# One flag of the tile scheduler: the same instructions, ordered by its timeline model instead of its core model

## The chip, the core and the metric

The kernel runs on one core of a Trainium2 chip. The time is that of one execution on the device, in microseconds (us). A NeuronCore has five engines with a queue each, taken in order: PE (TensorE, matmuls; PEld is its weight load), ACT (ScalarE), DVE (VectorE), POOL (GpSimd) and SP (SyncE, which here issues the DMAs).

## The reference

One inference step of one encoder layer, in float32, for 1024 tokens of a new prompt and 64 tokens of a stream that has 512 tokens in its caches:

```
h = x + 0.5 * rmsnorm(swiglu(rmsnorm(x, g_pre1), w_gate1, w_up1, w_down1), g_post1)
u = rmsnorm(h, g_premix) @ w_in      # split: c_q, c_kv, k_r | q_sb, k_sb, v_sb
o_mla = 8 heads of latent attention  # low-rank q and kv, rotary key, causal by chunks of 64
o_sb  = 8 heads of stick-breaking attention:
        z = q k * scale;  a = exp(log_sigmoid(z) + sum over later visible keys of log_sigmoid(-z))
h = h + rmsnorm(concat(headnorm(o_mla), headnorm(o_sb)) @ w_out, g_postmix)
h = h + 0.5 * rmsnorm(swiglu(rmsnorm(h, g_pre2), w_gate2, w_up2, w_down2), g_post2)
y = rmsnorm(h, g_final)              # and the new cache rows are returned
```

The width is 1024, the feed-forward width 2816.

## The kernel before

Features lie on the partitions, tokens on the moving axis. The tokens are two groups: group 1 holds 576 (the first half of the prompt and the sample, moved in chunks of 288), group 2 the other 512 (one chunk of 512). A float32 product is made of three matmuls of split operands (mm3, line 158: hi x hi, hi x lo, lo x hi), so each weight tile is loaded, split into wh and wl (lines 121 and 122) and used three times per chunk. Line 133 is the one line that issues every matmul, line 137 every transpose; so in the trace a matmul is told apart by its output tile.

The program writes two streams of work and weaves them. The mixing stream is, for one group, the end of the first feed-forward block (finish), the norm and input projections (premix, project), the attention (attend), and the output projection with its norm and residual (mix_out). Its PSUM tiles are called v, t and s, one buffer each (pool psa). The feed-forward stream computes the SwiGLU blocks (ffn, line 245); its PSUM tiles are called f, four buffers (pool psf). There are four feed-forward blocks in a row: the first of group 1, which runs alone (to about 430 us); block1, the first of group 2, woven with mix0, the mixing of group 1; block2, the second of group 1, woven with mix1, the mixing of group 2; block3, the second of group 2, at the end. Block2 needs the result of mix0 (prep2 scales it as its input), block3 that of mix1.

The weave (line 149) hands out the written order: after each step of the mixing stream it lets the feed-forward stream run until it has made SHARE times as much TensorE work:

```python
            while self.debt > 0 and next(second, None):
                self.debt -= self.work - mark
                mark = self.work
```

The written order is not yet the order on the engines. The tile context takes the whole program and schedules it: for each engine it takes, at each point of a modelled time, the instruction that is first in the written order among those whose operands and buffers are ready by the model. That fixes each engine's queue before the kernel runs; on the chip every engine takes its queue in order and waits where it must.

In the attention, a step computes the scores of 128 queries against n keys into the one tile s (scores, line 499), and then, for the stick-breaking heads (stick, line 510): a mask added on DVE (line 663), Abs, Exp and Ln on ACT (lines 517 to 519, of which 518 and 519 work on the copy a), a minimum with s on DVE (line 520), and one or two scans on DVE that read s again (lines 526 and 529). After the last reader of s the next scores may be written. The weights a are then turned by transposes into t, split (lines 563, 564) and multiplied with the values into v (weighted, line 545). The feed-forward stream's own VectorE work stands beside it: line 265 adds a down projection from f to y.

Of the kernel before, what the change touches and what calls it, by code (L numbers as in the profile page):

```python
# [15 lines left out]
P = 128  # L16
# [18 lines left out]
# token groups: (first token, tokens, chunk of the moving axis). The tokens lie as  # L35
# the first half of the prompt, the sample, the second half of the prompt.
# [4 lines left out]
# TensorE work of the feed-forward stream for one unit of the mixing stream's, part by part  # L41
# [8 lines left out]
class Layer:  # L50
    def __init__(self, tc, ctx, a):
        self.tc, self.nc, self.a = tc, tc.nc, a
        nc = self.nc
        self.const = ctx.enter_context(tc.tile_pool(name="const", bufs=1))
        nc.scalar.preload_act_table_set("natural_log_exp_and_others")
        self.turn = 0
        self.work = self.share = self.debt = 0.0
        self.pace = PACE
        self.mixed = False
        self.psf = ctx.enter_context(tc.tile_pool(name="psf", bufs=4, space=PSUM))  # L60
        self.psa = ctx.enter_context(tc.tile_pool(name="psa", bufs=1, space=PSUM))
        self.dram = ctx.enter_context(tc.tile_pool(name="dram", bufs=1, space=DRAM))
        c = self.const

        def load(name, shape, dt=F32):
            t = c.tile(list(shape), dt, name="c_" + name)
            nc.sync.dma_start(t, a[name])
            return t

        self.ones = c.tile([P, P], F32, name="ones")  # L70
        nc.vector.memset(self.ones, 1.0)
        self.eps = c.tile([P, 1], F32, name="eps")
        nc.vector.memset(self.eps, EPS)
        self.one = self.ones[:, 0:1]
        self.load = load

        def scratch(name, shape):
            return self.dram.tile(list(shape), F32, name=name)

        self.h1 = [scratch(f"h1_{g}", [P, KT, T]) for g, (_, T, _) in enumerate((G1, G2))]  # L80
        self.h2 = scratch("h2", [P, KT, G1[1]])
        self.o_s = [scratch(f"o_{g}", [D, T]) for g, (_, T, _) in enumerate((G1, G2))]
        self.qm = [scratch(f"qm_{g}", [HEADS, P, T]) for g, (_, T, _) in enumerate((G1, G2))]
        self.qs = [scratch(f"qs_{g}", [512, T]) for g, (_, T, _) in enumerate((G1, G2))]
        # keys and values: group 1 (prompt | new), group 2, cached
        self.kn = [scratch(f"kn_{g}", [512, T]) for g, T in enumerate((576, 512, 512))]
        self.kr = [scratch(f"kr_{g}", [32, T]) for g, T in enumerate((576, 512, 512))]
        self.ks = [scratch(f"ks_{g}", [512, T]) for g, T in enumerate((576, 512, 512))]
        self.vm = [scratch(f"vm_{g}", [T, 512]) for g, T in enumerate((576, 512, 512))]
        self.vs = [scratch(f"vs_{g}", [T, 512]) for g, T in enumerate((576, 512, 512))]  # L90
# [23 lines left out]
    # x = hi + lo exactly; without x, lo holds the value and is replaced in place  # L114
# [12 lines left out]
    # TensorE work is counted, for the interleaving of the two streams  # L127
# [15 lines left out]
    # a step without TensorE work in the first stream makes room for some of the second's  # L143
# [4 lines left out]
    # the steps of the first stream, with the second one's between them: self.share of its work each  # L148
# [15 lines left out]
    # a bank of the feed-forward stream  # L164
# [3 lines left out]
    # a bank of the mixing stream  # L168
# [10 lines left out]
    # sum of squares, tile by tile  # L179
# [9 lines left out]
    # 1 / sqrt(mean over all features + eps), on every partition, from the sums of squares  # L189
# [9 lines left out]
    # the same with the sums over the tiles left to TensorE (T at most 512)  # L199
# [10 lines left out]
    # tmp() gives [P, T] tiles  # L210
# [9 lines left out]
    # hi and lo of gain * src * r  # L220
# [7 lines left out]
    # y := res + gain * y * r, for one tile of features  # L228
# [76 lines left out]
    # projections of the mixing block for the tokens of one group  # L305
    def project(self, gi, g, hi, lo, pool, ev, tmp):
        nc, a = self.nc, self.a
# [13 lines left out]
        # query latent  # L321
# [13 lines left out]
        # rotary key: rows 64..95 the key, rows 96..127 its halves swapped  # L335
# [14 lines left out]
        # stick-breaking queries and keys, two heads per tile  # L350
# [16 lines left out]
        # latent attention: queries  # L367
        for m in range(2):
            # four heads: [query tile][head][128]
            wh, wl = self.weight(pool, a["wuq"][m])  # L370
            for h in range(4):
                e = tmp()
                for c0 in range(0, T, C):
                    cs = slice(c0, c0 + C)
                    ps = self.bank_m()
                    yield
                    for k in range(2):
                        ws = slice((k * 4 + h) * P, (k * 4 + h) * P + P)
                        self.mm3(ps[:, :C], wh[:, ws], wl[:, ws], cqh[:, k, cs], cql[:, k, cs], k == 0, k == 1)
                    nc.vector.tensor_tensor(e[:, cs], ps[:, :C], tab[:, cs], op=ALU.mult)  # L380
                nc.sync.dma_start(self.qm[gi][4 * m + h], e)
        # key/value latent
# [14 lines left out]
        # stick-breaking values, tokens on the partitions  # L397
# [17 lines left out]
        # latent attention: keys and values  # L415
# [3 lines left out]
    def cached(self, pool, ev, tmp):  # L419
        """keys and values of the cached latents"""  # L420
        nc, a = self.nc, self.a
        wh, wl = self.weight(pool, a["wukv"])
        cal = ev.tile([P, PAST], F32R, name="ll")
        cah = ev.tile([P, PAST], F32R, name="lh")
        ca = tmp()[:, :PAST]
        nc.sync.dma_start(ca, a["c_lat"])
        self.split(cah, cal, x=ca)
        yield from self.latent_kv(ev, tmp, wh, wl, cah, cal, PAST, PAST, 2)
# [25 lines left out]
    # ---- attention pieces  # L454
    def load_keys(self, pool, kind, h, parts):
        """hi and lo of the keys of one head on 128 rows."""
# [19 lines left out]
    def load_values(self, pool, pair, parts):  # L476
        """[128 keys, key tile, head, hi|lo, 64]"""
# [21 lines left out]
    def scores(self, ops, n):  # L499
        """ops: list of (lhsT, rhs tile); n keys in one or two equal halves."""  # L500
        nh = 1 if n <= 512 else 2
        w = max(n // nh, 256)
        ps = self.psa.tile([P, 2, 512], F32, name="s")
        for hf in range(nh):
            for i, (l, r) in enumerate(ops):
                self.mul(ps[:, hf, :w], lhsT=l, rhs=r[:, hf * w:hf * w + w],
                                      start=i == 0, stop=i == len(ops) - 1)
        return ps, nh, n // nh

    def stick(self, pool, ps, nh, w, n, mask):  # L510
        """weights of stick-breaking attention from the scores; the last key is never visible."""
# [9 lines left out]
        # minus the log weight: v[j] = (z[j+1] + v[j+1]) - log_beta[j]  # L521
# [23 lines left out]
    def weighted(self, pool, ab, v, h, tiles, o, par):  # L545
        """o[64*par .., 256] = sum over keys of value * weight, for two blocks of queries; the first block
        does not see the last tile of keys."""
# [40 lines left out]
    def headnorm(self, pool, o, n, row, gi, c0, sums=None, turned=None):  # L588
        """per-head RMSNorm of two heads on the partitions; sums or turned: eps * (softmax sum)^2 of each query."""
# [88 lines left out]
    def sum_rows(self, pool, total, nb):  # L678
        """eps * sum^2 of each query, repeated over the 64 rows of its head."""
# [9 lines left out]
    def sample_pair(self, pool, kind, pair):  # L689
# [9 lines left out]
        for par in range(2):  # L699
# [6 lines left out]
            # queries of this head in its own half of the columns, zeros in the other  # L706
# [54 lines left out]
        if mla:  # L761
            # row r of lhsT holds query r % 64 of head r // 64: only its own head's rows count
# [8 lines left out]
    # output projection, post norm, the residual (left in y), and the statistics of the next norm  # L771
# [30 lines left out]
def body(tc, a, ctx):  # L802
# [6 lines left out]
    # pool of the feed-forward stream  # L809
# [28 lines left out]
    def finish(gi, y, n, bank):  # L838
        """post norm and residual of a feed-forward block; after the second the final norm"""
# [18 lines left out]
    def last(gi, y, res, pool, step):  # L858
        """the same in steps of tokens, with the residual at hand"""
# [22 lines left out]
    def work(pool, T, n=4):  # L882
        """tiles for passing use, weights, and accumulators of the mixing stream"""
        class W:
            def tile(self, shape, dt, name):
                return pool.tile(shape, dt, name=name, bufs=2)
        return lambda: pool.tile([P, T], F32, name="e", bufs=n), W(), lambda: pool.tile([P, T], F32, name="acc")

    # first feed-forward block of group 1; the input norm of group 2 lies beside it
    T1, T2 = G1[1], G2[1]  # L890
    x1 = pair(fp, T2, "x")
    with tc.tile_pool(name="x0", bufs=1) as xp:
# [5 lines left out]
        for c0 in (0, half):  # L898
# [9 lines left out]
            # what the first half of the tokens suffices for  # L908
# [104 lines left out]
def layout(inp):  # L1013
    """The arrays of the launch: the inputs in the order the chip reads them, and constants of the shapes."""
# [14 lines left out]
    def tiles(w):  # [K, M] -> [M/128][128, K/128 * 128]  # L1029
# [22 lines left out]
    # constants  # L1052
# [15 lines left out]
def build(nc, arrays):  # L1068
# [5 lines left out]
    with tile.TileContext(nc) as tc:  # L1074
# [23 lines left out]
```

## Time and profile before

| | |
|---|---|
| median of 3 runs | 2368.2 us (2366.61 to 2371.72) |
| profiled execution, span from first to last instruction (no other time of it is given) | 2367.6 us |
| PE busy | 2283.5 us, 96% |
| DVE busy | 1539.0 us, 65% |
| ACT busy | 1244.7 us, 53% |
| POOL busy | 93.6 us, 4% |
| granted clock of TensorE, mean | 0.993 |

The profile is one execution. Busy time is that of an engine's instructions; a share of the span is a mean over stages. The granted clock is in parts of TensorE's full speed, 2.4 GHz; 0.50 is 1.2 GHz. In the views by windows each row is a stretch of the span.

### The profile page before, as it was taken

What the parts mean: (1) busy time and instruction counts of PE and PEld (TensorE: products, weight loads), DVE (VectorE), ACT (ScalarE), POOL (GpSimd) and SP (SyncE); (2) the same over time, 40 slices, a digit from 0 to 9 for tenths busy, and PEclk for the clock granted to TensorE, in tenths of its full rate; (3) what the DMA queues carried; (4) which work ended last, traced back from release to release, by engine and by line L of the source; (5) the groups of instructions that cost most, each with busy time, mean ns of one, the idle gap of its engine ahead of it and who ended that gap; (6) DMA issues with size and microseconds to landing.
All of it is one profiled execution on the core that took longest, in us unless ns stands there. A gap on an engine that the chain in (4) does not pass through costs nothing.

```text
span 2367.6 us, 37687 instructions
## 1 busy us (share of the span) xinstructions
PE 2283.5 (96%) x13869; PEld 2033.4 (86%) x13869; DVE 1539.0 (65%) x2743; ACT 1244.7 (53%) x2459; POOL 93.6 (4%) x270
## 2 busy tenths in 40 slices
PE   8999999989999999999999999999999999999997
PEld 7999999879987777788778999998888888888885
DVE  5555555764277878855873488888878588555555
ACT  6543333453367777754542477777776455433333
POOL 1000000010000000000110000000000010000001
PEclk9999999999999999999999999999999999999998
DMA  6322222445453343343444632323221424333321
GB/s 210 97 95 90 81 80 90 148 144 168 161 150 113 110 129 100 95 151 111 151 142 160 188 96 79 99 72 99 72 86 62 144 81 139 128 98 98 98 90 36
DMA packets 186615, 268.81 MB, mean 114 GB/s; under 512 B 59216, under 2 KB 68048, under 8 KB 186400
## 3 DMA queue, kind: packets, MB, share of 16 engines
q1 hardware_dynamic: 186432, 266.41, 35.8%
q8 instruction: 110, 1.80, 0.3%
q14 instruction: 73, 0.60, 0.1%
HBM read 227.61 MB, written 40.88 MB: 113 GB/s over the span
## 4 chain that ended last, share of the span: by engine, by line
PE 69%; DVE 12%; ACT 9%; DMA 4%; issue 4%; SPq 1%; POOL 1%; DVEq 0%; ACTq 0%; POOLq 0%
PE f L133 46%; PE s L133 11%; PE v L133 6%; PE t L133 3%; PE t L137 2%; DVE a L526 2%; DVE a L529 1%; ACT wh L121 1%; DVE a L520 1%; ACT a L517 1%; DVE wl L122 1%; ACT a L518 1%; ACT a L519 1%; DVE y L265 1%; DVE e L224 1%
## 5 line engine op out<-in xcount | busy, mean ns | idle before, releaser
L133 PE MATMUL f<-xh,wh 128*128 128x288 f32 (+1 forms) x2112 | 695.3, 329 | 4.4 <-ACT xh L121 2.8
L133 PE MATMUL f<-xl,wh 128*128 128x288 f32 (+1 forms) x2112 | 694.3, 329 | 2.9 <-POOL xl L122 1.8
L133 PE MATMUL f<-xh,wl 128*128 128x288 f32 (+1 forms) x2112 | 692.8, 328 | 0.0
L121 ACT CAST wh<-wr 128x512 fp32r<-128x512 f32 x638 | 374.2, 617 | 524.9 <-PE f L133 376.5
L122 DVE TENSOR_TENSOR wl<-wr,wh 128x512 fp32r<-128x512 f32 x638 | 431.2, 698 | 233.0 <-ACT wh L121 208.7
L133 PEld LDWEIGHTS f<-xl,wh 128*128 128x128 f32 x2112 | 397.7, 188 | 33.7 <-POOL xl L122 3.4
L133 PEld LDWEIGHTS f<-xh,wh 128*128 128x128 f32 x2112 | 397.6, 188 | 33.3 <-ACT xh L121 3.3
L133 PEld LDWEIGHTS f<-xh,wl 128*128 128x128 f32 x2112 | 397.5, 188 | 28.1 <-issue 0.8
L133 PE MATMUL f<-hh,wh 128*128 128x288 f32 (+2 forms) x1072 | 350.7, 328 | 6.6 <-ACT hh L121 3.2
L133 PE MATMUL f<-hl,wh 128*128 128x288 f32 (+2 forms) x1072 | 350.7, 327 | 0.0
L133 PE MATMUL f<-hh,wl 128*128 128x288 f32 (+2 forms) x1072 | 349.9, 327 | 0.2 <-DVE wl L122 0.2
L265 DVE TENSOR_TENSOR y<-f,y 128x288 f32<-128x288 f32 (+2 forms) x488 | 247.9, 523 | 85.4 <-PE f L133 83.8
L133 PEld LDWEIGHTS f<-hh,wh 128*128 128x128 f32 x1072 | 201.7, 189 | 23.4 <-ACT hh L121 4.0
L133 PEld LDWEIGHTS f<-hh,wl 128*128 128x128 f32 x1072 | 202.1, 189 | 14.3 <-issue 1.0
L133 PEld LDWEIGHTS f<-hl,wh 128*128 128x128 f32 x1072 | 202.1, 189 | 13.8 <-issue 0.8
L293 DVE TENSOR_TENSOR act<-f,act 128x288 f32<-128x288 f32 (+1 forms) x132 | 70.0, 531 | 92.6 <-PE f L133 91.8
L564 DVE TENSOR_TENSOR pl<-t,ph 128x384 fp32r<-128x384 f32 (+1 forms) x160 | 101.2, 633 | 35.6 <-ACT ph L563 31.2
L563 ACT CAST ph<-t 128x384 fp32r<-128x384 f32 (+1 forms) x160 | 86.7, 542 | 57.2 <-PE t L137 54.7
L292 DVE TENSOR_TENSOR act<-f,act 128x288 f32<-128x288 f32 (+1 forms) x132 | 69.8, 529 | 66.5 <-ACT act L291 66.4
L137 PE MATMUL t<-c_ident,a 128*128 128x128 f32 x616 | 106.0, 277 | 2.7 <-ACT a L531 0.9
L133 PE MATMUL s<-kh,qh 128*128 128x256 f32 (+3 forms) x224 | 84.4, 378 | 24.0 <-DVE a L529 16.1
L121 ACT CAST hh<-act 128x288 fp32r<-128x288 f32 (+1 forms) x132 | 64.8, 491 | 66.0 <-DVE act L293 65.9
(312 smaller groups left out, 3464.7 us busy)
## 6 DMA issues: line engine op xcount, KB each, us to landing
wr<-in_wg SPq DMA_DIRECT2D x176, 256.0 KB, 2.9
wr<-in_wu SPq DMA_DIRECT2D x176, 256.0 KB, 3.0
wr<-in_wd SPq DMA_DIRECT2D x176, 256.0 KB, 3.2
wr<-in_win SPq DMA_DIRECT2D x44, 256.0 KB, 3.3
kl<-ks SPq DMA_DIRECT2D x64, 128.0 KB, 2.8
wr<-in_wout SPq DMA_DIRECT2D x32, 256.0 KB, 2.8
h<-y SPq DMA_DIRECT2D x16, 288.0 KB, 2.3
p<-in_xT SPq DMA_DIRECT2D x16, 256.0 KB, 3.4
```

The lines of the kernel that those rows point to most:

```text
L121: nc.scalar.copy(hi, x)
L122: eng.tensor_tensor(lo, x, f(hi), op=ALU.subtract)
L133: self.nc.tensor.matmul(out, lhsT=lhsT, rhs=rhs, start=start, stop=stop)
L137: self.nc.tensor.transpose(out, x, ident)
L224: self.nc.vector.scalar_tensor_tensor(x, src(k), self.gain(name, k), r, op0=ALU.mult, op1=ALU.mult)
L265: nc.vector.tensor_tensor(yy, ps[:, :C], yy, op=ALU.add)
L292: nc.vector.tensor_tensor(s, pg[:, :C], s, op=ALU.mult)
L293: nc.vector.tensor_tensor(s, pu[:, :C], s, op=ALU.mult)
L517: nc.scalar.activation(av, z, AF.Abs)
L526: nc.vector.tensor_tensor_scan(a[:, j0:n - 1][:, ::-1], zz[:, ::-1], a[:, j0:n - 1][:, ::-1], BIG, op0=ALU.add, op1=ALU.subtract)
L563: nc.scalar.copy(ph[:, end:], tr[:, end:])
L564: nc.vector.tensor_tensor(pl[:, end:], tr[:, end:], f(ph[:, end:]), op=ALU.subtract)
```

## The change

The tile context is opened with a flag. Its scheduler then takes the time at which an instruction is ready from its timeline model, where it took it from its core model. The rest of the diff removes comments, without moving a line.

```diff
@@ -1071,7 +1071,7 @@
     for k, s in OUTS.items():
         a[k] = nc.dram_tensor("out_" + k, list(s), F32, kind="ExternalOutput").ap()
     a["xT"] = [a["xT0"], a["xT1"]]
-    with tile.TileContext(nc) as tc:
+    with tile.TileContext(nc, schedule_with_timeline_sim=True) as tc:
         with ExitStack() as ctx:
             body(tc, a, ctx)
```

The instructions are the same, 13688 on PE, 1247 on SP and 275 on POOL in both programs; 26 copies that may go to any engine move from DVE to ACT (2745 and 2393 before, 2719 and 2419 now). Their order differs on every engine. Numbers behind a tile's name count the tiles in the written order, the same in both programs.

First place: TensorE, in the attention of group 1, at the step v_8434 (the product of weights and values of one pair of heads). The tiles f_9278 and f_12538 belong to block1; f_12538 is its last one. In the order before:

```order
L133 MATMUL f_9278<-xl_99,wh_9257 128x512
L133 MATMUL f_9278<-xh_98,wl_9256 128x512
L133 MATMUL v_8434<-pl_8437,v_8382 128x256
L133 MATMUL v_8434<-ph_8436,v_8382 128x256
...
L133 MATMUL f_9278<-xh_98,wh_9257 128x512
```

And in the new order:

```order
L133 MATMUL f_12538<-hh_12372,wh_12443 128x512
L133 MATMUL f_12538<-hl_12373,wh_12443 128x512
L133 MATMUL f_12538<-hh_12372,wl_12442 128x512
L133 MATMUL v_8434<-pl_8437,v_8382 128x256
L133 MATMUL v_8434<-ph_8436,v_8382 128x256
...
L133 MATMUL s_8561<-kh_8550,qh_8556 128x256
L133 MATMUL s_8561<-kl_8549,qh_8556 128x256
L137 MATMUL t_8507<-c_ident_988,a_8497 128x128
```

Block1's matmuls from f_9278 to f_12538 stood behind v_8434 and now stand ahead of it; what follows v_8434 is scores and transposes of the attention.

Second place: TensorE, in the attention of group 2, at the transposes t_17196. The tiles f_18505 and f_21639 belong to block2; f_21639 is its last one. In the order before:

```order
L133 MATMUL f_18505<-xl_12460,wh_18427 128x288
L133 MATMUL f_18505<-xh_12459,wl_18426 128x288
L137 MATMUL t_17196<-c_ident_988,a_17156 128x128
L137 MATMUL t_17196<-c_ident_988,a_17108 128x128
...
L133 MATMUL v_17161<-pl_17176,v_16743 128x256
L133 MATMUL v_17161<-ph_17175,v_16743 128x256
...
L133 MATMUL s_17251<-kh_17079,qh_17089 128x512
```

And in the new order:

```order
L133 MATMUL f_21639<-hh_21381,wh_21510 128x288
L133 MATMUL f_21639<-hl_21382,wh_21510 128x288
L133 MATMUL f_21639<-hh_21381,wl_21509 128x288
L137 MATMUL t_17196<-c_ident_988,a_17156 128x128
L137 MATMUL t_17196<-c_ident_988,a_17108 128x128
...
L133 MATMUL v_17161<-pl_17176,v_16743 128x256
L133 MATMUL v_17161<-ph_17175,v_16743 128x256
...
L133 MATMUL s_17464<-kh_17451,qh_17459 128x320
L133 MATMUL s_17464<-kl_17450,qh_17459 128x320
```

Block2's matmuls from f_18505 to f_21639 now stand ahead of t_17196, and so does the score matmul s_17251, which followed it.

## Rows read from the trace of the kernel before

**Rows 1.** The page: span, and busy time, share of the span and instructions by engine.

```profile
span 2367.6 us, 37687 instructions
...
PE 2283.5 (96%) x13869; PEld 2033.4 (86%) x13869; DVE 1539.0 (65%) x2743; ACT 1244.7 (53%) x2459; POOL 93.6 (4%) x270
```

**Rows 2.** Windows, feed-forward alone: length, busy (count) by engine, clock, DMA share, GB/s.

```profile
core 0: us, PE busy (x) PEld busy (x) DVE busy (x) ACT busy (x) POOL busy (x), PEclk, DMA share, GB/s
118.40:177.60 59.20, 59.20 (x448) 59.20 (x448) 31.68 (x61) 24.19 (x52) 2.69 (x2) 1.00 0.30 95
2131.20:2190.40 59.20, 59.20 (x263) 48.99 (x262) 31.38 (x49) 20.25 (x37) 0.00 (x0) 1.00 0.31 98
```

**Rows 3.** Windows, only instructions on tile s: PE, PEld, DVE, ACT busy.

```profile
798.69:1026.75 228.06, 31.42 (x138) 20.62 (x138) 54.93 (x114) 22.82 (x60) 1.00 0.37 109
1622.59:1836.64 214.05, 30.59 (x118) 19.08 (x118) 64.76 (x82) 23.58 (x36) 1.00 0.24 75
```

**Rows 4.** Timeline of one turn of s: start, duration, engine, line, operation [wait].

```profile
893.87 0.47 PE L133 MATMUL s<-kh,qh 128*128 128x512 f32 x1 [0.25 <-DVE a L526]
...
898.16 0.69 DVE L265 TENSOR_TENSOR y<-f,y 128x512 f32<-128x512 f32 x1
...
900.13 0.35 PE L133 MATMUL s<-kh,qh 128*128 128x256 f32 x1 [0.42 <-DVE a L526]
```

**Rows 5.** Windows, only PE's instructions on tiles f.

```profile
798.69:1026.75 228.06, 159.62 (x619) 1.00 0.37 109
1026.75:1096.66 69.91, 17.32 (x75) 1.00 0.36 118
1096.66:1160.80 64.14, 59.22 (x252) 1.00 0.46 143
1622.59:1836.64 214.05, 138.19 (x951) 1.00 0.24 75
1836.64:1902.29 65.65, 19.86 (x142) 1.00 0.39 128
1902.29:1966.77 64.48, 57.97 (x409) 0.97 0.30 90
```

**Rows 6.** Windows, all instructions, columns as in rows 2.

```profile
430.00:798.69 368.69, 357.24 (x2097) 307.24 (x2095) 229.27 (x423) 198.49 (x425) 16.73 (x57) 1.00 0.47 148
798.69:1026.75 228.06, 221.44 (x1133) 173.94 (x1133) 180.03 (x360) 166.06 (x369) 10.73 (x73) 1.00 0.37 109
1026.75:1096.66 69.91, 69.74 (x465) 65.30 (x463) 32.00 (x51) 28.10 (x53) 0.00 (x0) 1.00 0.36 118
...
1160.80:1622.59 461.79, 446.54 (x2949) 409.35 (x2948) 331.44 (x571) 283.57 (x531) 18.53 (x62) 0.99 0.40 123
1622.59:1836.64 214.05, 203.11 (x1449) 189.77 (x1448) 172.04 (x303) 151.11 (x266) 6.13 (x42) 1.00 0.24 75
1836.64:1902.29 65.65, 63.80 (x337) 55.01 (x335) 32.81 (x57) 25.19 (x46) 0.00 (x0) 1.00 0.39 128
...
0.00:34.46 34.46, 25.68 (x103) 19.34 (x104) 20.11 (x38) 20.89 (x48) 8.18 (x12) 0.90 0.69 230
```

**Rows 7.** Timeline, PE: two score matmuls, and two sums of squares behind the residuals.

```profile
809.18 0.36 PE L133 MATMUL s<-kh,qh 128*128 128x256 f32 x1 [0.38 <-DVE a L526]
...
1136.17 0.75 PE L133 MATMUL s<-rx,ones 128*128 128x288 f32 x2 [2.21 <-DVE rx L187]
...
1628.94 0.39 PE L133 MATMUL s<-kh,qh 128*128 128x320 f32 x1
...
1931.88 0.65 PE L133 MATMUL t<-rx,ones 128*128 128x512 f32 x1
```

**Rows 8.** Groups on tile a from 798.69: count, then min/median/max ns.

```profile
L518 ACT ACTIVATE a<-a x25: 309/527/707, 798.3 to 1014.0; 128x384 f32<-128x384 f32 x6, 128x512 f32<-128x512 f32 x6, 128x128 f32<-128x128 f32 x5, 128x256 f32<-128x256 f32 x5
L519 ACT ACTIVATE a<-a,ones x25: 400/617/780, 798.9 to 1015.2; 128x384 f32<-128x384 f32 x6, 128x512 f32<-128x512 f32 x6, 128x128 f32<-128x128 f32 x5, 128x256 f32<-128x256 f32 x5
```

**Rows 9.** Windows around two drops of the granted clock, columns as in rows 2.

```profile
1192.00:1199.00 7.00, 2.50 (x18) 2.22 (x18) 7.00 (x12) 3.69 (x8) 1.44 (x1) 0.87 0.72 228
1199.00:1203.00 4.00, 4.00 (x12) 2.97 (x13) 2.97 (x7) 2.79 (x6) 0.00 (x0) 0.50 0.68 221
...
17.00:20.00 3.00, 2.97 (x9) 2.41 (x10) 3.00 (x7) 2.58 (x7) 1.45 (x2) 0.50 0.00 0
```

## The prediction

> **The bound.** I read the page first: TensorE is busy in 2283.5 us of a span of 2367.6 [rows 1]. That 96% would make any order of the same instructions worth nothing, and it is a mean over stages with different limits, so I went on to the windows. In two stretches that hold feed-forward work alone, TensorE is never idle and a matmul takes 59.20/448 = 0.132 us with 288 columns and 59.20/263 = 0.225 us with 512 [rows 2]. These are the prices of feed-forward work wherever it stands.
>
> Then I read the attention stretches by tile. The score tile s has one buffer, and it is handed from a score matmul to the mask, three ScalarE passes, a VectorE minimum and a scan, and only then to the next score matmul. Instructions on that tile alone take 31.42 us on TensorE, 54.93 on VectorE and 22.82 on ScalarE of the 228.06 us of group 1's last part of attention [rows 3]. One turn shows the pace: score matmul at 893.87, next at 900.13, started when the scan of line 526 ended, 6.26 us later, and in the turn stands one VectorE addition of the feed-forward stream, 0.69 us, between the steps of the chain [rows 4]. So attention advances at the pace of a chain in which TensorE has a small part, and TensorE reads as full only because feed-forward matmuls fill the rest of every turn. The reader should see two limits that lie on each other: TensorE's work and the score chain.
>
> **The change.** No instruction's work is added or removed; some 26 copies go from VectorE to ScalarE, which at about the 0.69 us of the addition in rows 4, on engines that other work keeps free for them, I cost at nothing (ends: 18 us either way, if all lay on one engine's path). What changes is the order. The two pieces of the order ahead show it: TensorE takes block1's feed-forward matmuls up to the last one (f_12538) before the attention step v_8434, and block2's up to the last one (f_21639) before t_17196. In the trace of before those steps start at 798.69 and 1622.59, and after them stand 619 + 75 + 252 = 946 feed-forward matmuls of block1 and 951 + 142 + 409 = 1502 of block2 [rows 5]. In the new order these lie ahead of that point, and behind it the attention goes on with nothing to fill its turns; the next block can't fill them, since block2 needs the result of mix0 and block3 that of mix1.
>
> *Work pulled ahead.* 946 x 0.2251 = 212.9 us, and 1502 x 0.1321 = 198.5 us. It is put into stretches where TensorE is already busy 357.24 of 368.69 us and 446.54 of 461.79 [rows 6], so there is room for 11.45 and 15.25 us at most. I take 8 and 10 as filled (ends: 0 and all of it). VectorE can follow: 229.27 us there, and 946/263 x 31.38 = 113 us more, in 574 us of time. The weights of the pulled matmuls are loaded ahead with them, on SP's queue; the DMA share is 0.31 in the dense stretch and 0.47 here, so neither is full.
>
> *What is left of the first stretch.* From 798.69 to 1160.80 were 362.1 us. In the new order they are replaced by four pieces in a row. The attention: the next score matmul in the new order is s_8561, which starts at 809.18 in the trace [rows 7], so 1026.75 - 809.18 = 217.6 us of attention remain. Without feed-forward work its turns get shorter. The one turn above gives (6.26 - 0.69)/6.26 = 0.89. The floor is the chain's own instructions with every hand-over at zero: 31.42 + 54.93 + 22.82 and the two passes of lines 518 and 519 that touch only its copy, 25 x (0.527 + 0.617) = 28.6 [rows 8], together 137.8 of 228.06, which is 0.60. The other end is 1.0. I take 0.85, near the turn, which has its hand-overs in it: 184.9 us. The output projection: 69.91 us [rows 6], with 17.32 us of feed-forward work in it [rows 5], of which I take off half (ends: none and all): 61.3. The statistics and the residual, one tile after another through a load, to the matmul at 1136.17: 40.3 [rows 7], TensorE hardly works there. The scaling of the next block's input, 8 tiles, each a multiplication and a split of about 0.7 us (the addition in rows 4 is the nearest): 10. Sum 296.5, so 65.6 us go. First stage: 212.9 - 8 - 65.6 = +139.3.
>
> *The second stretch* alike, from 1622.59 to 1966.77, 344.2 us: the attention from 1628.94 [rows 7] to 1836.64, 207.7 x 0.85 = 176.5; the projection 65.65 less half of 19.86, 55.7; the statistics to 1932.5, 30.2; the scaling 10. Sum 272.4, so 71.8 go. Second stage: 198.5 - 10 - 71.8 = +116.7.
>
> *The clock.* Around 1192 to 1199 TensorE is busy 2.50 us of 7.00, and in the next 4 us, busy throughout, its granted clock is 0.50, the level of 1.2 GHz; at the start of the kernel a like drop is seen [rows 9]. In the bare attention TensorE will be used as lightly: the matmuls that are not feed-forward take 221.44 - 159.62 = 61.8 us there, a third of 184.9. If all score matmuls of both stretches ran at half the clock, 31.42 + 30.59 = 62.0 us would be added; at full clock nothing. I take 10, since the matmuls there come every few us and the drops in the trace are short.
>
> The Trainium skill ("TensorE: Matmul & The Clock Gate", Part 1, on the gate) says that the throttled state is the default and that activity releases it. By the row alone the drop is an episode, and the sum stands; by the rule a lightly used engine stays throttled, and the sum would be 52 us higher. The trace bears the rule out in its direction: 0.50 behind a light stretch, 1.00 in every dense one. No row shows a long light stretch.
>
> *The start of the kernel.* The new order also exchanges weights and tokens of the first 35 us. TensorE is idle for 34.46 - 25.68 = 8.8 us there [rows 6]; ends: that much less, that much more; I take zero.
>
> *Sum:* 139.3 + 116.7 + 10 = +266.0 on the profiled span of 2367.6, which is 0.6 under the median of the runs: 2633.6, 2634 us. Nothing moves in the last block, which starts later by the whole sum.
>
> **Rivals.**
>
> *The clock stays low in both bare stretches.* The price is the 52 us not yet counted: 2686 us. For it: the rows at the low level, behind TensorE busy 36% [rows 9]. Against it: that light stretch itself was still granted 0.87 on average, and in the turns of the attention matmuls come a few us apart. Chance 0.13.
>
> *The bare chain is much faster,* because most of each turn is waiting behind feed-forward work on ScalarE and VectorE: a factor of 0.65 in place of 0.85, 0.20 x 425.3 = 85 us less, 2549. For it: the floor of 0.60. Against it: the turn of rows 4 holds one feed-forward operation between the chain's steps. Chance 0.07.
>
> *TensorE is the only bound, and the new order serves it better: faster.* The filled idle time, 11.45 + 15.25 = 26.7 us, would be won, and the attention behind would run at TensorE's own share, 61.8 and 203.11 - 138.19 = 64.9 us: 2341. It decides from where the bare attention takes no more than these 127 us of its 425, a factor of 0.30. Against it: half of the floor of the chain. Chance 0.03.
>
> *The order doesn't matter,* since the sum of TensorE's work is the same and the engines' queues even it out: 2368. TensorE takes its instructions in order, and the displaced ones depend on nothing that could slide back. Chance 0.02.
>
> **The numbers.** The forecast has 0.75. Its own range: factor 0.75 to 1.0 (-43 to +64), half of the projection's overlap (18.6 either way), recovered idle time (-9 to +18), the start (8.8 either way), the clock (-10 to +52). Not all fall on one side, so 2570 to 2725, which also holds the rival of the clock; outside lie the other three and a little of the upper end, some 0.17. A measurement of this kernel tells 0.2% (5 us) from no change. Faster by over that: 0.03, the third rival; within: 0.02; slower: 0.95.
>
> **Signs.** In the changed kernel's windows: a stretch of about 180 us in either attention without a single feed-forward matmul, TensorE busy about a third there; before it stretches at 97% and more that are 205 and 188 us longer; block2's first feed-forward matmul near 1300 (1160.80 now) and block3's near 2230 (1966.77 now). The granted clock in the bare stretches separates the first rival; the time of a turn, 5.3 us where it was 6.26, the second. The prediction is wrong if feed-forward matmuls run beside the attention to its end.

## The result, and the profile after

The changed kernel takes 2735.83 us (median of 4 runs, 2733.68 to 2737.0) where the kernel before takes 2368.24: a ratio of 1.1545, interval 1.1528 to 1.1561. The forecast was slower, 2634 us, with a range that ended at 2725; the loss is 367.6 us where 266 were forecast. Of the four runs of e8, below, one took 4615 us, and the time given for e8 is the median of the other three.

The page of the changed kernel, span and busy time as in [rows 1]:

```profile
span 2733.3 us, 37804 instructions
...
PE 2369.9 (87%) x13869; PEld 2129.1 (78%) x13869; DVE 1536.0 (56%) x2717; ACT 1272.0 (47%) x2485; POOL 102.3 (4%) x270
```

The other engines work as long as before. TensorE is busy 86 us longer at the same instructions, and idles 363 us where it idled 84. The windows of the changed kernel on tile f, as in [rows 5], show where:

```profile
430.00:1003.52 573.52, 400.37 (x1734) 0.99 0.42 132
1003.52:1339.48 335.96, 0.00 (x1) 0.63 0.22 66
1339.48:1993.23 653.75, 451.99 (x3168) 0.99 0.36 111
1993.23:2327.77 334.54, 0.00 (x0) 0.67 0.17 51
```

Two stretches of 336 and 335 us hold no feed-forward matmul. They begin with v_8434 (1003.52, was 798.69) and t_17196 (1993.23, was 1622.59) and end with the first matmul of block2 (1339.48, was 1160.80) and of block3 (2327.77, was 1966.77). The same stretches with all engines, as in [rows 6]; of each the attention, the projection, and the statistics with the scaling:

```profile
430.00:1003.52 573.52, 565.52 (x3069) 492.15 (x3068) 339.38 (x599) 281.34 (x571) 17.62 (x59) 0.99 0.42 132
...
1006.17:1224.77 218.60, 130.96 (x508) 101.01 (x508) 110.66 (x240) 113.98 (x270) 10.30 (x69) 0.58 0.18 48
1224.77:1294.83 70.06, 54.59 (x386) 53.94 (x387) 21.67 (x32) 25.98 (x50) 0.00 (x0) 0.86 0.32 103
1294.83:1339.48 44.65, 4.71 (x9) 1.98 (x9) 17.18 (x24) 9.87 (x17) 2.79 (x2) 0.50 0.29 93
1339.48:1993.23 653.75, 639.12 (x4450) 611.75 (x4450) 436.33 (x785) 360.95 (x691) 24.52 (x64) 0.99 0.36 111
1997.14:2214.10 216.96, 120.24 (x485) 98.29 (x486) 112.59 (x168) 108.77 (x168) 6.47 (x42) 0.64 0.09 26
2214.10:2282.62 68.52, 50.71 (x199) 38.90 (x200) 21.37 (x32) 25.84 (x44) 0.00 (x0) 0.83 0.33 104
2282.62:2327.77 45.15, 5.75 (x9) 1.72 (x8) 32.03 (x45) 15.39 (x27) 12.02 (x4) 0.56 0.23 74
2327.77:2733.30 405.53, 380.86 (x1696) 316.41 (x1696) 210.54 (x336) 146.16 (x268) 14.20 (x12) 0.97 0.27 89
```

The reader should see three things. Ahead of the bare stretches TensorE is full, at 98.6 and 97.8%. In the bare attentions VectorE is busy about half the time and ScalarE about half, and still they take 218.6 and 217.0 us, where the same steps with all the feed-forward work between them took 217.6 and 207.7 before. And the granted clock there is 0.58 and 0.64 in the mean, between the levels of 1.2 and 2.4 GHz; TensorE is busy 60 and 55% of the time, where the prediction's sign was a third.

On the score tile alone, the same steps before (809.18 to 1026.75 and 1628.94 to 1836.64) and in the changed kernel:

```profile
809.18:1026.75 217.57, 30.72 (x136) 20.29 (x136) 51.25 (x109) 22.24 (x59) 1.00 0.36 106
1628.94:1836.64 207.70, 28.88 (x112) 18.06 (x112) 63.43 (x80) 22.27 (x32) 1.00 0.24 74
```

```profile
1006.17:1224.77 218.60, 47.16 (x136) 32.17 (x136) 51.58 (x109) 22.18 (x59) 0.58 0.18 48
1997.14:2214.10 216.96, 42.82 (x112) 29.41 (x112) 63.81 (x80) 22.17 (x32) 0.64 0.09 26
```

VectorE and ScalarE spend the same time on it; TensorE spends 16.4 us more in the first attention and 13.9 in the second, at the lower clock. What is left between in the first, 217.57 - 104.21 = 113.4 us before, is 97.7 now: 15.7 us less. The two nearly cancel. Waits of TensorE in the first bare attention (waiter, what it waited for, us in total, times, longest):

```profile
PE s L133 <- DVE a L526: 39.9, 14, 5.7
PE t L137 <- DVE pl L564: 14.4, 8, 2.2
```

The score matmul waits for the scan, as it did before, but in the kernel before feed-forward matmuls filled these waits.

### The profile page after: what moved, and what is told of

It reads as the page before. It is cut to its first block, busy times and chain, and to the rows that moved or that the text cites. A ratio compares the mean times of both kernels' runs of the same rounds, so it can differ in the third digit from the quotient of the medians.

```text
span 2733.3 us, 37804 instructions
## 1 busy us (share of the span) xinstructions
PE 2369.9 (87%) x13869; PEld 2129.1 (78%) x13869; DVE 1536.0 (56%) x2717; ACT 1272.0 (47%) x2485; POOL 102.3 (4%) x270
## 5 line engine op out<-in xcount | busy, mean ns | idle before, releaser
L121 ACT CAST wh<-wr 128x512 fp32r<-128x512 f32 x638 | 362.5, 618 | 598.6 <-PE f L133 420.5
L122 DVE TENSOR_TENSOR wl<-wr,wh 128x512 fp32r<-128x512 f32 x638 | 417.4, 692 | 365.5 <-ACT wh L121 359.1
L137 PE MATMUL t<-c_ident,a 128*128 128x128 f32 x616 | 129.2, 329 | 71.9 <-DVE pl L564 51.8
L133 PE MATMUL s<-kh,qh 128*128 128x256 f32 (+3 forms) x224 | 100.3, 449 | 86.9 <-DVE a L529 40.5
L137 PEld LDWEIGHTS t<-c_ident,a 128*128 128x128 f32 x616 | 89.8, 167 | 100.4 <-DVE pl L564 32.7
L133 PE MATMUL v<-pl,v 128*128 128x256 f32 x320 | 113.2, 369 | 24.0 <-DVE pl L564 18.0
```

What stands on the lines that cost most here:

```text
L121: nc.scalar.copy(hi, x)
L122: eng.tensor_tensor(lo, x, f(hi), op=ALU.subtract)
L133: self.nc.tensor.matmul(out, lhsT=lhsT, rhs=rhs, start=start, stop=stop)
L137: self.nc.tensor.transpose(out, x, ident)
```

## Experiments

All were run beside the kernel before, whose median was 2366 to 2369 us each time; ratios are to it.

**e1: the work written ahead, core model.** The shares are changed, no flag.

```diff
-SHARE = (0.1, 1.5, 0.1, 0.1, 1.2, 0.1)
+SHARE = (0.35, 8.0, 0.1, 0.3, 4.0, 0.1)
```

> The core model orders the program, as in the kernel before; only the weave's shares are changed, so that the feed-forward stream is written as far ahead of the mixing stream as the new order has it (its matmuls of block1 and block2 end in the first and in the second attention at about the same step). Theory A (feed-forward work taken ahead leaves the rest of the attention bare, and that alone is the loss): 2700 to 2750 us, with two stretches of about 330 us without a feed-forward matmul. Theory C (the loss comes from something else in the new order: VectorE, ScalarE or the DMA queue): under 2450 us.

2763.8 us (1.168, 1.1663 to 1.1698). Its windows on tile f:

```profile
1009.60:1357.90 348.30, 0.00 (x0) 0.63 0.21 64
2012.60:2360.00 347.40, 0.00 (x0) 0.69 0.17 54
```

The time is 14 us over the range of theory A, and theory C is far off. The old scheduler model makes a loss of the same kind and a little more when the feed-forward stream is written as far ahead. Being far ahead is enough, without the flag.

**e2: the stream held back, with the flag.**

```diff
+        elif self.side == 2 and len(self.lead) > 0:
+            self.tc.add_manual_dep(ins.ins, self.lead[-1].name, mybir.DependencyInfo(
+                mybir.DependencyClass.NoSync, mybir.DependencyReason.DATA), reason="order")
-SHARE = (0.1, 1.5, 0.1, 0.1, 1.2, 0.1)
+SHARE = (0.1, 2.35, 0.1, 0.1, 1.75, 0.1)
```

> The flag stays on; each feed-forward matmul that is written between two steps of the mixing stream is queued behind the last mixing matmul written before it, and the shares of the two attentions are raised from 1.5 and 1.2 to 2.35 and 1.75, so that TensorE has the feed-forward work where the kernel before has it. All other engines keep the order that the timeline model gives. Theory A: 2350 to 2400 us. Theory C: over 2600 us.

2654.7 us (1.1216): theory A missed. The first attention took 467 us (711 to 1178) where it took 351 before (690 to 1041), with TensorE busy 381 and 343 of them. Either the ties leave TensorE's order worse than before, or the other engines' order costs; the run can't tell which, so the next pair ties the order exactly.

**e5, e6, e9 to e11: whole queues tied.** A table holds the order of an engine's instructions in one kernel; each is tied behind the one before it.

```diff
+    d = np.frombuffer(zlib.decompress(base64.b85decode(order)), np.int16).astype(int)
+    at = np.cumsum(d + 1) - 1
+    for p, q in zip(at, at[1:]):
+        tc.add_manual_dep(mine[q], mine[p].name, mybir.DependencyInfo(
+            mybir.DependencyClass.NoSync, mybir.DependencyReason.DATA), reason="order")
```

> The flag stays on, but TensorE's matmuls and transposes are tied, each behind the one before it, into exactly the order of the kernel before (a table of 13686 numbers); ScalarE, VectorE, GpSimd and the DMA queue are ordered by the timeline model around it. Theory A (TensorE's order alone makes the loss): 2360 to 2400 us. Theory C (the order that the timeline model gives the other engines makes the loss, as the 2655 us of the kernel with the stream held back would have it): 2600 to 2740 us. A number between them splits the loss.

> The reverse: the core model, with TensorE tied into exactly the order of the changed kernel. Theory A: 2700 to 2750 us. Theory C: under 2450 us.

> The flag with TensorE and ScalarE tied into the order of the kernel before; VectorE, GpSimd and the DMA queue are left to the timeline model. With TensorE alone tied it took 2551 us. Theory D1 (the 184 us left there come from ScalarE's queue: passes of the score chain behind work that isn't ready): under 2420 us. Theory D2 (they come from VectorE's queue): over 2500 us. Theory D3 (from the DMA queue, or both alike): between, or over 2500 in the next run too.

> The flag with TensorE and VectorE tied into the order of the kernel before; ScalarE, GpSimd and the DMA queue are left to the timeline model. D1: over 2500 us. D2: under 2420 us. D3: neither.

> The flag with TensorE, ScalarE and VectorE tied into the order of the kernel before; GpSimd, the DMA queue and the engine of 95 free copies are left to the timeline model. D1 and D2: 2360 to 2385 us. D3 with the DMA queue: over 2450 us.

| model | queues tied | us | ratio |
|---|---|---|---|
| flag | none (the changed kernel) | 2735.8 | 1.1545 |
| core (e6) | TensorE as in the changed kernel | 2730.9 | 1.1534, 1.1515 to 1.1554 |
| flag (e5) | TensorE as before | 2551.4 | 1.0779, 1.0758 to 1.0801 |
| flag (e9) | TensorE, ScalarE as before | 2476.9 | 1.0470, 1.0451 to 1.0488 |
| flag (e10) | TensorE, VectorE as before | 2481.5 | 1.0490, 1.0472 to 1.0507 |
| flag (e11) | all three as before | 2374.8 | 1.0037, 1.0023 to 1.0051 |

With TensorE's new order the time is within 5 us of the changed kernel's, whichever model orders the rest (e6, theory A): TensorE's order is enough to make the loss. The other engines were not held at their old order there; the core model laid theirs around TensorE's. Giving TensorE its old order back wins only half of the loss (e5, between the two theories): the order that the timeline model gives the other engines around it, which is not their order in the changed kernel either, costs 184 us. Some 70 to 75 of these go with ScalarE's old order alone or VectorE's alone, and all but 8 with both (theory D3, both alike). So either cause makes a loss by itself, and the two lie on each other and don't add. The waits of TensorE show the second, in the kernel before and in e5:

```profile
PE s L133 <- DVE a L529: 16.1, 26, 2.0
PE s L133 <- DVE a L526: 6.5, 18, 0.6
```

```profile
PE s L176 <- DVE a L572: 40.6, 19, 5.1
PE t L180 <- DVE pl L607: 29.0, 30, 3.4
...
PE s L176 <- DVE a L569: 16.7, 14, 2.9
```

At the same order of matmuls the scans that release the score tile come later: 57.3 us of waits where there were 22.6, and 29.0 on the split of the turned weights where there was 0.5. That is some 63 of the 178 us between the two profiled spans; the rest was not followed. What delays a scan can be read in the turn of [rows 4], which takes 7.43 us in e5 (929.94 to 937.37) where it took 6.26. VectorE's queue there (lines are 43 further down):

```profile
933.46 0.68 DVE L563 SCALAR_TENSOR_TENSOR a<-s,a 128x512 f32<-128x512 f32 x1
934.80 0.69 DVE L165 TENSOR_TENSOR kl<-kl,kh 128x512 fp32r<-128x512 f32 x1 [0.66 <-ACT kh L164]
935.41 0.69 DVE L308 TENSOR_TENSOR y<-f,y 128x512 f32<-128x512 f32 x1
936.01 1.21 DVE L569 TENSOR_TENSOR_SCAN a<-s,a 128x511 f32<-128x511 f32 x1
```

Between the minimum and the scan stands the split of the next keys, kl, which waits 0.66 us for ScalarE's part of it (kh); in the kernel before only the addition stood there.

**e3: 8 needless matmuls a step, in the score tile.**

```diff
+            for i in range(8):
+                self.nc.tensor.matmul(ps[:, 1], lhsT=ops[0][0], rhs=ops[0][1][:, 0:512], start=i == 0, stop=i == 7)
```

> The changed kernel with 8 needless matmuls of 512 columns behind each score step of group 1 from the 32nd on, into the half of the score tile that these steps leave empty; nothing reads them. They only keep TensorE busy (1.7 us a step at full clock). Theory A1 (the lower granted clock, 0.58 in the first bare attention, is why that stretch is 218.6 us and not 185): the clock there rises over 0.9, the stretch falls to 175 to 195 us, the whole to 2690 to 2715 us. Theory A2 (the turn of the score tile has its length from ScalarE and VectorE, whatever TensorE's clock): the stretch stays within 212 to 226 us, the whole 2728 to 2745 us.

2784.7 us (1.1766), neither theory. The timeline of one step shows that the design was at fault:

```profile
1099.59 3.10 PE L511 MATMUL s<-kh,qh 128*128 128x512 f32 x8
...
1102.73 0.30 DVE L667 TENSOR_TENSOR s<-s,c_tri 128x128 f32<-128x128 f32 x1 [2.88 <-PE s L511]
```

The mask waits for the needless matmuls, though it touches another half of the tile: the framework orders by whole tiles. They lengthened the chain in place of filling it, and the run says nothing of the clock.

**e4: two score steps in the halves of one tile.**

```diff
+        if share and self.other is not None:
+            ps, self.other = self.other[:, 1:2], None
```

> The changed kernel, but two score steps of a head of group 1 share one score tile, a half each, so that a score matmul need not wait for the scan of the step before it. Theory A (the hand-over of the one score tile sets the pace of the bare attention): the first bare stretch falls from 218.6 to 140 to 185 us, the whole to 2655 to 2700 us; the second stretch, of group 2, where a step fills both halves, stays at 217 us. If not the tile but the engines' own order sets the pace: 210 us and more in the first too, 2725 to 2740 us.

2734.1 us (1.1552), no change, and for the same reason: the matmul into the second half (of a head's four steps the fourth, 512 keys) still waits for the scan on the first (the third, 384 keys).

```profile
1110.14 0.95 DVE L532 TENSOR_TENSOR_SCAN a<-s,a 128x383 f32<-128x383 f32 x1
...
1111.14 0.79 PE L134 MATMUL s<-kh,qh 128*128 128x512 f32 x1 [1.24 <-DVE a L532]
```

So e4 says nothing of the bank. Both were made again with a bank of their own.

**e8 and e12: a second score bank**, taken from the feed-forward stream, for every second step of group 1; e8 with the flag, e12 with the core model.

```diff
-tc.tile_pool(name="psf", bufs=4, space=PSUM))
+tc.tile_pool(name="psf", bufs=3, space=PSUM))
+        if odd:
+            ps = self.psx.tile([P, 1, 512], F32, name="x")
```

> The changed kernel with three feed-forward banks, and the fourth as a second score tile for every second step of group 1, so that a score matmul need not wait for the scan of the step before it. If the hand-over of the one score tile sets the pace of the bare attention: the first bare stretch falls from 218.6 to 140 to 195 us, the whole to 2660 to 2715 us. If it doesn't (ScalarE's and VectorE's queues carry the steps one after another anyway): 208 us and more.

> The kernel before (core model) with three feed-forward banks and the fourth as a second score tile for every second step of group 1. The bank is one of two limits that lie on each other, TensorE's work is the other, so the attention of group 1 has little to gain: 2345 to 2370 us. If three banks are too few for the feed-forward stream: over 2380 us.

e8: 2669.0 us (1.1272, 1.1253 to 1.1291), 58 us under the kernel with three banks and no second score bank (e13, below). In the new order block1's work also reaches further into the attention, to 1039, so the bare stretches are compared from v_9553 on to the second chunk of the projection, in the changed kernel and in e8:

```profile
1123.20:1239.00 115.80, 68.28 (x249) 52.82 (x249) 52.92 (x113) 56.58 (x132) 3.85 (x25) 0.53 0.19 58
```

```profile
1087.70:1181.50 93.80, 57.29 (x237) 45.09 (x237) 48.95 (x105) 52.87 (x126) 3.80 (x25) 0.63 0.24 71
```

19% shorter at a clock still low, with the same wait of 13 us for the projection's operands in both rows: the hand-over of the one score tile sets the pace of much of the bare attention, as expected. With the core model (e12) the same edit takes 2382.9 us (1.0067), in the range that was expected if three banks are too few. So it shows that the edit as a whole wins nothing in the old order; what the second score tile alone is worth there was not tried apart from the lost bank.

**e7, e13, e14: the clock.** e13 is the changed kernel with three feed-forward banks. In e7 and e14 needless matmuls go to the fourth bank, tied into TensorE's queue where the changed kernel waits: 344 in the first attention (e7), 1117 in both bare stretches (e14).

```diff
+        px = L.psx.tile([P, 512], F32, name="x")
+        for _ in range(sum(k for _, k in BEFORE)):
+            FILL.append(nc.tensor.matmul(px[:, :P], lhsT=L.ident, rhs=L.ones, start=True, stop=True).ins)
...
+    for p, k in reversed(BEFORE):
+        at[p:p] = [len(mine) + i for i in range(n - k, n)]
```

> The changed kernel with three in place of four feed-forward banks, and 344 needless matmuls (float32, 128 columns, 0.2 us each at full clock) into the fourth bank, which nobody reads, put into TensorE's order where the trace of the changed kernel shows it waiting in the first bare attention, 0.8 of each wait; the order is tied otherwise. Theory A1 (the lower granted clock keeps the bare stretch from getting shorter): the clock there is over 0.9 where it was 0.58, and the stretch falls from 218.6 to 175 to 200 us. Theory A2 (the clock costs it little, the chain through ScalarE and VectorE sets its length): over 208 us at whatever clock.

> The changed kernel with three in place of four feed-forward banks and nothing else: what the filled kernel is to be compared with. 2715 to 2755 us; the part of the first attention behind block1's last matmul within 5 us of the changed kernel's, and its granted clock under 0.7.

> The same with 1117 needless matmuls in both stretches without feed-forward work, from the step behind block1's last matmul to block2's first, and from the step behind block2's last to block3's first, 0.8 of each wait that the changed kernel's trace shows on TensorE. Theory A1 (the clock is most of what the forecast missed, near 75 us): 60 us and more under the kernel with three banks. Theory A2 (the clock is worth little, the chain's own length was misjudged): less than 20 us under it. Between: 3.5% of each stretch per 20 us.

e7 took 2719.6 us (1.1479), e13 2727.0 (1.152), e14 2714.6 (1.146). TensorE's own matmuls stand in the same order in e13 and e14. The windows from s_8861 to the second chunk of the projection, and from t_17953 to the statistics, in e13 and in e14:

```profile
1035.20:1235.30 200.10, 114.71 (x459) 87.81 (x460) 99.78 (x217) 105.41 (x249) 8.48 (x56) 0.60 0.21 59
2069.20:2263.30 194.10, 122.49 (x518) 97.55 (x517) 86.94 (x131) 89.33 (x145) 4.28 (x26) 0.74 0.15 50
```

```profile
1036.80:1225.00 188.20, 156.23 (x1169) 140.77 (x1170) 99.25 (x217) 104.99 (x249) 8.37 (x56) 0.99 0.22 63
2068.50:2252.20 183.70, 159.46 (x1055) 140.75 (x1053) 87.29 (x131) 90.00 (x147) 3.96 (x26) 0.99 0.17 54
```

The granted clock rises from 0.60 and 0.74 to 0.99, and the stretches lose 11.9 and 10.4 us, 6% and 5%. That is a lower bound, since some of the needless matmuls stand in the way. The whole gains only 12.4 us, so some 10 of the 22.3 are lost again elsewhere; where was not traced. By the whole it is theory A2, the clock is worth little; how short the chain is at the full clock with nothing in its way no run shows. In e7 the same first stretch took 189.0 us at a clock of 0.96, like e14's. The same steps took 200.7 us in the kernel before, with all the feed-forward work between them.

## Why the prediction was wrong

The mechanism was right in its outline: work pulled ahead, the attention left bare, and no overlap in between. What failed is the step that shortens the stretches left bare, in the attention and in the projection. The sum, term by term, in us:

| term | forecast | measured |
|---|---|---|
| pulled ahead, first (with what was filled) | +204.9 | +204.8 |
| pulled ahead, second | +188.5 | +192.0 |
| attention left bare, first | 184.9 | 218.6 |
| attention left bare, second | 176.5 | 217.0 |
| projections | 61.3 and 55.7 | 70.1 and 68.5 |
| statistics, residual and scaling | 50.3 and 40.2 | 44.7 and 45.2 |
| from the border to the next score matmul | not counted | 2.7 and 3.9 |
| block3 and the end | 0 | +4.7 |
| clock | +10 | in the rows above |

**Pulled ahead.** This is the largest term, and it could be had from the order and two windows. That it came out to 0.1 and 3.5 us is in part luck. TensorE's busy time ahead of the border grew by 565.52 - 357.24 = 208.3 and 639.12 - 446.54 = 192.6 us, where 212.9 and 198.5 were forecast; and of the idle time there 3.4 and 0.6 us were filled, where 8 and 10 were taken. The two misses offset each other.

**The factor of 0.85 failed.** It was mis-sized: 1.005 and 1.045 were measured (218.6 of 217.6, 217.0 of 207.7). That is 33.7 + 40.5 = 74.2 of the 99.7 us between 2633.6 and the span of 2733.3. At the full clock it is 188.2 of 200.7, or 0.94, for most of the first stretch (e14, with some needless matmuls in the way). So the 0.85 had two faults: at most 0.94 - 0.85 = 0.09 is the chain's own length, and at least 0.06 is the clock. The first comes from taking the factor from one turn, [rows 4], and from the premise that the place of a feed-forward addition stays empty once it is gone. That same turn got longer in the changed kernel, 7.02 us, where 5.3 were forecast:

```profile
1086.16 0.77 PE L133 MATMUL s<-kh,qh 128*128 128x512 f32 x1 [1.35 <-DVE a L526]
...
1090.14 0.69 DVE L520 SCALAR_TENSOR_TENSOR a<-s,a 128x512 f32<-128x512 f32 x1 [1.40 <-ACT a L519]
1090.56 0.62 ACT L121 CAST kh<-kl 128x512 fp32r<-128x512 f32 x1 [0.51 <-DMA kl<-kr]
...
1091.21 0.69 DVE L122 TENSOR_TENSOR kl<-kl,kh 128x512 fp32r<-128x512 f32 x1 [0.38 <-ACT kh L121]
1091.82 1.21 DVE L526 TENSOR_TENSOR_SCAN a<-s,a 128x511 f32<-128x511 f32 x1
...
1093.18 0.55 PE L133 MATMUL s<-kh,qh 128*128 128x256 f32 x1 [5.61 <-DVE a L526]
```

Where the addition stood, between the minimum and the scan, now stands the attention's own split of the next keys, which waits for a DMA; in the kernel before it stood behind the scan. The turn takes 6.99 us in e13 and in e14, so the clock is not the reason. In e6, where the core model orders VectorE and the scan follows the minimum at once, it takes 6.07 us (1101.69 to 1107.77), still over 5.3. This is one turn; since e6 on the whole is within 5 us of the changed kernel, what this one gains must be lost elsewhere.

**The clock** was forecast at 10 us, its rival at 62. The rival was right on the state: 0.58 and 0.64 in the mean of both attentions. The price lies between. The score matmuls did not double: TensorE spent 16.4 + 13.9 = 30.3 us more on them, and e14 against e13 puts at least 22.3 us on the longer part of both stretches. The Trainium skill ("TensorE: Matmul & The Clock Gate", Part 1, on the gate) says that the throttled state is the default and that activity releases it. The traces agree, with 0.60 bare (e13) and 0.99 filled (e14) in the first stretch. The 61.8 us of TensorE's other work in the first attention was too low: it is a difference of busy times that overlap, and by tile (s, t and v) the matmuls from 809.18 on alone had taken 30.72 + 22.94 + 41.85 = 95.5 us.

**The projections** were forecast with half of the feed-forward work in them taken off. Nothing came off: they took 70.1 and 68.5 us where they took 69.9 and 65.7 with that work in them [rows 6]. That is 21.6 us, and here the overlap was misread. Both projections begin with a wait for the reloaded output of the attention and the first weights (line 121 makes their halves). Feed-forward matmuls filled it in the kernel before, on tile f:

```profile
1026.75:1040.62 13.87, 13.87 (x61) 1.00 0.71 248
1836.64:1854.34 17.70, 15.56 (x114) 1.00 0.60 204
```

In the changed kernel the same wait stands bare, and is as long:

```profile
1224.77:1238.39 13.62, 0.69 (x3) 0.50 (x3) 6.08 (x9) 6.62 (x12) 0.00 (x0) 0.50 0.61 214
2214.10:2231.57 17.47, 2.08 (x3) 0.50 (x3) 5.99 (x10) 6.87 (x12) 0.00 (x0) 0.50 0.51 166
```

So 29.4 of the 37.2 us of feed-forward work lay in a wait, and taking them out shortens nothing. The clock plays a small part: behind the wait the projections take 56.6 and 50.2 us in e13 and 55.8 and 49.6 in e14.

**The statistics.** The scaling took 6 us and not 10 in the first. In the second the end of the other group's block, which had been beside feed-forward work later, now stands in the same place: its sums on TensorE at 2316.82 and 2325.30 lie among the last steps.

```profile
2316.82 1.32 PE L133 MATMUL v<-tmp,ones 128*128 128x288 f32 x2 [33.18 <-DVE tmp L187]
...
2325.30 1.33 PE L133 MATMUL t<-tmp,ones 128*128 128x288 f32 x2 [0.78 <-ACT rx L196]
```

**The other rivals.** The chain that is much faster bare (0.65) is not seen in any run; with a second bank the part compared above took 93.8 us, where the same steps took 114.1 in the kernel before, a factor of 0.82. That TensorE is the only bound falls with the bare attention's 218.6 us at 131 us of work. That the order doesn't matter falls with the result, and with e6 for TensorE's order.

**The range.** It held the ends of each term, but counted on their not falling on one side. The factor and the projections both came out past their upper ends (1.0, and nothing taken off), and, as far as the rows above show, for a like reason: feed-forward work that lay in a wait takes no time off when it goes.

**What the prediction left out.** It costed the order of VectorE and ScalarE at nothing. On the whole that did not spoil the sum, since e6 comes within 5 us of the changed kernel with another order on both. Where TensorE keeps its old order, the timeline model's order of the others costs 184 us by itself (e5).

No kernel here beats the one before. Why the timeline model's order of ScalarE and VectorE delays the scans (e5) was followed to single instructions in one turn only.

## What to carry to other kernels

A queue that is 96% busy can still be two limits lying on each other. If work that fills another chain's waits is moved ahead of it, the price is nearly the whole of that work: count the moved instructions, and assume that the chain gets no shorter until the mean of all its turns, not one of them, says otherwise. Ask of each piece of the moved work whether it stood in the chain's way or in one of its waits. A scheduler's order is a property of all queues together: tying one engine back undid half of the loss, tying three undid it.

## What the runs showed of the hardware

The granted clock stayed at 0.58 in the mean over the 218.6 us of the bare attention, with TensorE busy 131 us in short pieces. Over most of the same steps it was 0.60 in e13, and 0.99 in e14 with needless matmuls in TensorE's waits. The low clock cost at least 6% and 5% of the two stretches compared. The rest is of the framework and not of the chip: two halves of one PSUM tile are ordered as one (e3, e4).
